# Attention heads of the first mixer: a written order for TensorE, a longer gap in the latent heads' chains, and part of the output projection between their last steps

## The chip, the cores and the metric

The kernel runs on one core of a Trainium2 chip. The metric is device time of one execution in microseconds (us); lower is better. A core has four compute engines that work side by side, each through its own queue in order: TensorE (PE in the profile; its weight loads are shown as PEld), VectorE (DVE), ScalarE (ACT) and GpSimd (POOL). The sync engine (SP) issues the DMA transfers. An instruction at the head of a queue that waits for another engine or for a transfer holds everything behind it on its own engine.

## The reference

One step of a two-layer diffusion backbone on 128 context tokens and 128 latent tokens (`NT` = 256 columns in all), in float32 with a width of 2048. Layer 0 mixes with two groups of heads in parallel, layer 1 with differential attention, and each layer ends in a gated convolution MLP. What this change touches is the mixer of layer 0, after its input projection:

```python
qa = (rmsnorm(q_lat, g_q) @ w_q_up).reshape(b, t, MLA_HEADS, MLA_NOPE_DIM + MLA_ROPE_DIM)
...
kv = (ckv_all @ w_kv_up).reshape(b, s, MLA_HEADS, MLA_NOPE_DIM + MLA_V_DIM)
ka = jnp.concatenate([kv[..., :MLA_NOPE_DIM], krope_all ...], axis=-1)
va = kv[..., MLA_NOPE_DIM:]
out_a = softmax_attention(jnp.concatenate([qa_nope, qa_rope], axis=-1), ka, va, MLA_SCALE)
out_b = softmax_attention(qb, kb_all, vb_all, HEAD_SCALE)
out = jnp.concatenate([out_a.reshape(b, t, -1), out_b.reshape(b, t, -1)], axis=-1) @ w_out
```

There are 8 latent (MLA) heads, whose queries and keys come out of two low-rank products, and 8 grouped-query (GQA) heads, whose queries need a normalisation and a rotation ("rope"). Beside this, all scales and shifts of the layers are computed from a condition vector by a large matrix `w_ada` (its blocks are called units here).

## The kernel before

**Products.** A weight block of 128x128 is split into a high and a low part (`wh` by ACT, `wl` by DVE), the activations likewise, and each block costs three matmuls of 256 columns: `wh` with the high part, `wh` with the low part, `wl` with the high part. A `gemm` sums 4, 6 or 16 blocks in a PSUM bank (`acc`).

**The heads.** They are done in four pairs (h = 0, 2, 4, 6). For a pair come two products for the latent queries (18 matmuls each), one for their rotary part, then for each of two GQA heads its scores (`gqa`) and a product for the latent keys (12 matmuls of 384 columns), then 36 matmuls for the latent values, then the scores of the two latent heads (`mla_pair`). A head's chain is a generator, `head_ab`: row maxima on DVE (`mx`), their scaled negative on POOL (`nmx`), the exponentials on ACT, a reciprocal and two scalings on DVE (`p`); after two hooks the transposes of `p` on PE, after one more the product with the values, whose result is split into `hx`, the operand of the output projection. A hook is a call of `pump`, which stands after each product: it advances each chain by a step, issues some of the matmuls that sum `w_ada` units on PE, and advances a list of `w_ada` sums on DVE (class `Deep`, L525: one custom instruction of 1024 elements; its tiles `block`, `kvb` and `more` are filled by DMAs). How much is set by `RATE` and `SIDE`.

**Query preparation.** `gqa_query(h + 1)` is started before the scores of head h. Its second step issues two small matmuls (`misc`) and the rotation of that head's query, five instructions on DVE. The scores of head h + 1 need it.

**PSUM banks.** Scores, transposes and value products share three banks (`att`), used in turn in the order in which the program asks for them. A tile thus waits until the tile three places before it has been read.

**Order.** In the heads the planner, which simulates the program, chooses the order on every engine from what it believes to be ready. Where `pe.in_turn` is set, PE keeps the order of the code (`keep_order`). In this stage it is not set.

**Output projection.** After the last chain (`flush`) `out_ab` loads three weight tiles and runs the first three of its 16 columns side by side (`first_three`), in the order `PAIR_LATE`: blocks 8 to 15, which are the GQA heads, then blocks 0 to 5, then 6 and 7, the last pair of latent heads. The planner is free to put parts of them between the last chains.

**Pushes.** In the mixer of layer 1, `push` makes two later matmuls wider than 256 columns after each attention step of a head: the first by 32 columns and the thirteenth by 16. The extra columns are not used.

## Time and profile before

| | |
|---|---|
| median of 3 runs | 2304.95 us (2304.35 to 2306.54) |
| the profiled execution | 2307.52 us, of which the span of instructions is 2305.7 us |
| PE busy | 2275.9 us (99%) |
| DVE busy | 1885.6 us (82%) |
| ACT busy | 1195.7 us (52%) |
| granted TensorE clock, mean | 0.993 |
| heads and first three output columns | about 203 to 357 us |
| output projection to its end | to about 438 us |

A row of the timeline gives start, length, engine, line, what is written and read, and how many instructions are merged in it. Matmuls overlap in the records, so what a matmul costs in a dense stretch is the distance from its start to the next start, and the lengths add up to more than the time. A window row gives the busy time of each engine in a stretch with the number of its instructions in brackets, then the granted TensorE clock (1.00 is full speed), the share of the DMA engines and GB/s. The line numbers are those of the kernel before; a short matmul in full float32 (scores, value products, `w_ada` sums) is written once in the code and appears twice in the trace.

### The profile page before, as it was taken

The page shows a single profiled execution, that of the slowest core. Times are in us where ns is not written, and L with a number is a line of the kernel's source. Part 1 is how long each engine was busy: PE and PEld are TensorE (multiplying, and loading weights), DVE is VectorE, ACT ScalarE, POOL GpSimd, SP SyncE. Part 2 cuts the span into 40 slices and gives each one's busy share as a digit, 9 for nine tenths or more (in the row PEclk, how much of TensorE's full clock was granted, in tenths as well). Part 3 has the DMA queues.
Part 4 walks back from the last instruction along what each step waited for, and adds up shares of the span by engine and source line. Part 5 has one row for each costly group of instructions (what it writes and reads, how often), then busy time and mean ns, then how long its engine had stood idle before and what let it go on. Part 6 is the DMA issues. An engine that isn't in the chain of part 4 may idle for free.

```text
span 2305.7 us, 47484 instructions
## 1 busy us (share of the span) xinstructions
PE 2275.9 (99%) x19496; PEld 2182.1 (95%) x19496; DVE 1885.6 (82%) x2973; ACT 1195.7 (52%) x1959; POOL 188.1 (8%) x238
## 2 busy tenths in 40 slices
PE   8999999999999999999999999999999999999998
PEld 6788878999999999999999999999999999999998
DVE  4667979989999999999978988898899965666654
ACT  4345555665553355555575455457555434555543
POOL 0002111300000000001130001023000000000011
PEclk9999999999999999999999999999999999999999
DMA  9987888777777777777788888776667755555553
GB/s 376 367 343 293 326 311 338 288 277 264 262 255 291 291 272 260 272 258 258 288 293 293 318 322 310 267 268 229 246 256 262 264 200 189 199 191 194 198 189 126
DMA packets 100122, 617.15 MB, mean 268 GB/s; under 512 B 10752, under 2 KB 18880, under 8 KB 33344
## 3 DMA queue, kind: packets, MB, share of 16 engines
q1 hardware_dynamic: 99904, 614.11, 72.2%
q8 instruction: 153, 2.51, 0.4%
q14 instruction: 65, 0.53, 0.1%
HBM read 609.32 MB, written 4.75 MB: 266 GB/s over the span
## 4 chain that ended last, share of the span: by engine, by line
PE 93%; DVE 3%; DMA 2%; issue 1%; POOL 1%; ACT 1%; SPq 0%; DVEq 0%; ACTq 0%; POOLq 0%
PE acc L110 86%; PE ada L110 3%; PE att L110 2%; DVE wl L249 1%; DVE hx L525 1%; DMA more<-w_ada 1%; PE att L113 1%; DMA raw<-w_out_c 0%; PE misc L110 0%; DMA araw<-w_ada 0%; DMA kvb<-w_ada 0%; POOL dev L807 0%; PE ada L113 0%; DVE rope L858 0%; ACT wh L248 0%
## 5 line engine op out<-in xcount | busy, mean ns | idle before, releaser
L110 PE MATMUL acc<-hx,wh 128*128 128x256 f32 (+1 forms) x7264 | 1255.2, 278 | 4.2 <-ACT wh L248 1.7
L248 ACT CAST wh<-raw 128x1024 fp32r<-128x1024 f32 (+1 forms) x834 | 796.6, 967 | 869.8 <-PE acc L110 736.6
L249 DVE TENSOR_TENSOR wl<-raw,wh 128x1024 fp32r<-128x1024 f32 (+1 forms) x834 | 925.4, 1126 | 246.9 <-ACT wh L248 240.2
L110 PEld LDWEIGHTS acc<-hx,wh 128*128 128x128 f32 x7264 | 1099.8, 188 | 23.2 <-ACT wh L248 8.1
L110 PE MATMUL acc<-hx,wl 128*128 128x256 f32 (+1 forms) x3632 | 1007.8, 278 | 5.3 <-DVE wl L249 5.1
L110 PEld LDWEIGHTS acc<-hx,wl 128*128 128x128 f32 x3632 | 684.5, 188 | 9.5 <-DVE wl L249 6.9
L110 PE MATMUL acc<-g,wh 128*128 128x256 f32 x2816 | 478.8, 276 | 0.0
L110 PEld LDWEIGHTS acc<-g,wh 128*128 128x128 f32 x2816 | 424.0, 188 | 0.0
L110 PE MATMUL acc<-g,wl 128*128 128x256 f32 x1408 | 388.1, 276 | 0.0
L473 DVE CUSTOM_DVE_ANT_0 junk<-araw,condb 128x2048 f32<-128x2048 f32 x128 | 294.4, 2300 | 0.0
L110 PEld LDWEIGHTS acc<-g,wl 128*128 128x128 f32 x1408 | 264.2, 188 | 0.0
L211 POOL TENSOR_TENSOR sqacc<-sqacc,sq 128x256 f32<-128x256 f32 x62 | 71.5, 1154 | 1491.1 <-ACT sq L207 1490.9
L110 PE MATMUL acc<-hxc,wh 128*128 128x256 f32 (+1 forms) x1056 | 189.3, 281 | 0.0
L110 PEld LDWEIGHTS acc<-hxc,wh 128*128 128x128 f32 x1056 | 161.9, 188 | 1.8 <-issue 1.7
L110 PE MATMUL acc<-hxc,wl 128*128 128x256 f32 (+1 forms) x528 | 146.9, 278 | 0.0
L110 PEld LDWEIGHTS acc<-hxc,wl 128*128 128x128 f32 x528 | 99.6, 189 | 0.2
L110 PE MATMUL acc<-wh,hxc 128*128 128x256 f32 (+1 forms) x512 | 95.0, 283 | 0.5 <-DVE nt L818 0.5
L1531 ACT ACTIVATE cv<-acc,convw 128x256 f32<-128x256 f32 x169 | 94.1, 557 | 0.0
L525 DVE CUSTOM_DVE_ANT_0 hx<-block,condb 128x1024 fp32r<-128x1024 f32 x65 | 79.3, 1221 | 7.3 <-DMA block<-w_ada 6.8
L1537 DVE SCALAR_TENSOR_TENSOR cv<-acc,convw,cv 128x254 f32<-128x254 f32 x169 | 81.1, 480 | 3.2
L843 DVE SCALAR_TENSOR_TENSOR x<-acc,mod,x 128x128 f32<-128x128 f32 x190 | 57.3, 344 | 31.6 <-PE acc L110 31.6
L110 PEld LDWEIGHTS acc<-wh,hxc 128*128 128x128 f32 x512 | 79.4, 188 | 3.4 <-issue 2.5
(263 smaller groups left out, 1800.4 us busy)
## 6 DMA issues: line engine op xcount, KB each, us to landing
raw<-w_up SPq DMA_DIRECT2D x176, 1024.0 KB, 4.8
araw<-w_ada SPq DMA_DIRECT2D x136, 1024.0 KB, 6.0
raw<-w_down SPq DMA_DIRECT2D x88, 1024.0 KB, 4.8
raw<-w_in_c SPq DMA_DIRECT2D x48, 1024.0 KB, 6.9
block<-w_ada SPq DMA_DIRECT2D x41, 512.0 KB, 6.8
raw<-w_in_ab SPq DMA_DIRECT2D x18, 1024.0 KB, 9.1
raw<-w_out_ab SPq DMA_DIRECT2D x16, 1024.0 KB, 7.9
raw<-w_out_c SPq DMA_DIRECT2D x16, 1024.0 KB, 7.1
```

The costliest lines, as they stand in the source:

```text
L110: return self.placed(nc.tensor.matmul(*a, **kw))
L113: return self.placed(nc.tensor.transpose(*a, **kw))
L211: eng.tensor_tensor(out=st["acc"], in0=st["acc"], in1=sq, op=ALU.add)
L248: pin(act.copy(out_hi, src))
L249: pin(dve.tensor_tensor(out=out_lo, in0=src, in1=out_hi.bitcast(F32), op=ALU.subtract))
L473: keep_order(dve.tensor_tensor_reduce(out=T_(feat["pool"], [P, D], "junk"), in1=feat["row"][:, c], in0=feat["raw"].rearrange("p g n -> p ( ...
L525: keep_order(dve.tensor_tensor_reduce(out=self.junk, in0=self.raw, in1=self.row[:, c].rearrange("p (g n) -> p g n", g=2), scale=1.0, scala ...
L843: dve.scalar_tensor_tensor(out=x[:, c, s], in0=ps[:, s], scalar=mod[:, l, 3 * which + 2, c, g:g + 1], in1=x[:, c, s], op0=ALU.mult, op1=AL ...
L1531: pin(act.activation(y, ps, AF.Identity, scale=cw[:, 1, m:m + 1], bias=cw[:, 3, m:m + 1]))
L1537: pin(dve.scalar_tensor_tensor(out=y3[:, :, :T - 1], in0=p3[:, :, 1:], scalar=cw[:, 2, m:m + 1], in1=y3[:, :, :T - 1], op0=ALU.mult, op1=A ...
```

## The change

1. In the heads `pe.in_turn` is set, so PE keeps the order of the code.
2. The chains of the latent heads wait three hooks instead of two before their transposes.
3. `first_three` becomes a class, `Three`. The three weight tiles of the output projection are loaded and two of them split in the last pair (h = 6). After the last scores PE runs 20 blocks (60 matmuls) of the output projection, then the last two heads' transposes, 4 more blocks, the last two value products, and the remaining 24 blocks. Between them stand four calls that advance the DVE sums, whose tile for unused results moves to `qb`.
4. The fourth weight tile of the output projection is loaded before that, and split in the first two of its columns (`W.ahead`).
5. `RATE` of the last quarter of the input projection goes from 0.25 to 0.3, of the heads from 0.72 to 0.62, of the output projection from 0.62 to 0.66: the same `w_ada` matmuls at other places.
6. The first push of layer 1 is 16 columns wide instead of 32.

```diff
-RATE = {"in0": 0.35, "in": 0.5, "in3": 0.25, "heads": 0.72, "out0": 0.62, "c": 0.36, "outc": 0.36}
+RATE = {"in0": 0.35, "in": 0.5, "in3": 0.3, "heads": 0.62, "out0": 0.66, "c": 0.36, "outc": 0.36}
...
-PUSH = [32] + 11 * [0] + [16]
+PUSH = [16] + 11 * [0] + [16]
...
+    class Three:
+
+        def __init__(self, W, xh, xl, order):
+            self.W, self.xh, self.xl, self.order = W, xh, xl, list(order)
+            self.raws = [W.load()[0] for _ in range(3)]
+            self.blocks, self.count, self.ps = {}, [0] * 3, []
+
+        def prepare(self, c, h):
+            self.blocks[c, h] = self.W.halves(self.raws[c], 8 * h)
+
+        def banks(self):
+            self.ps = [T_(pacc, [P, 512], "acc")[:, :NT] for _ in range(3)]
+
+        def run(self, n):
+            for _ in range(n):
+                c, k = self.order.pop(0)
+                if (c, k // 8) not in self.blocks:
+                    self.prepare(c, k // 8)
...
+        def even(self):
+            while isinstance(self.steps[0], partial) and self.steps[0].func == self.sums and self.steps[0].args[-1]:
                 self.step()
...
-    def head_ab(pl, s, rs, v, hx, c):
+    def head_ab(pl, s, rs, v, hx, c, wait=2):
...
-        yield
-        yield
+        for _ in range(wait):
+            yield
         pT = transposed(pl, p)
...
-                        start(head_ab(hp, s[i], rsm, lambda b, i=i: vm[:, b, i], o, h + i))
+                        start(head_ab(hp, s[i], rsm, lambda b, i=i: vm[:, b, i], o, h + i, 3))
...
+                pe.in_turn = True
                 for h in range(0, 8, 2):
...
+                    if h == 6:
+                        W = Weights(A["w_out_ab"], KD, 1)
+                        three = Three(W, lambda k: o[:, k, :NT], lambda k: o[:, k, NT:2 * NT], PAIR_LATE)
+                        three.prepare(0, 1)
+                        three.prepare(1, 1)
                     mla_pair(h, qr, kn, values())
-                flush()
+                deep.junk = qb[:, 0:4].rearrange("p (a b) n -> p a (b n)", a=2)
+                three.banks()
+                step()
+                three.prepare(2, 1)
+                three.prepare(0, 0)
+                for n in (6, 7, 7):
+                    three.run(n)
+                    deep.pump()
+                    if n == 6:
+                        step()
+                step()
+                three.run(4)
+                step()
+                deep.pump()
+                deep.even()
+                W.begun.append(W.load())
+                three.run(len(three.order))
+                pe.in_turn = False
...
-        ready = first_three(W, oh, ol, PAIR_LATE, first=1)
...
+            if c < 2:
+                W.ahead(lambda i: i)
```

In the rows of the changed kernel that follow, line numbers are its own (L883 and L884 are the maxima, L867 and L868 before).

PE, where the last GQA heads (6 and 7) end, before: `att_3682` and `att_3741` are their scores, `att_3773` the transposes of the first one's `p`, `ada_3623` a `w_ada` unit, `acc_3947` the first output column.

```order
L110 MATMUL att_3682<-kg_118,qb_242 128x128
L110 MATMUL att_3682<-kg_118,qb_242 128x256
L110 MATMUL att_3741<-kg_118,qb_242 128x128
L110 MATMUL att_3741<-kg_118,qb_242 128x256
L113 MATMUL att_3773<-cst_74,p_3687 128x128 x3
L110 MATMUL ada_3623<-araw_3632,condw_79 32x512 x4
L110 MATMUL ada_3623<-araw_3677,condw_79 32x512 x4
L110 MATMUL att_3823<-pT_3777,vg_119 128x128 x3
L113 MATMUL att_3829<-cst_74,p_3746 128x128 x3
```

PE, the end of the heads after the change: `acc_3918` is the third output column, `att_4001` and `att_4007` the transposes of the last two latent heads (ahead of them stand 24 matmuls each of the first two columns and 12 of the third, behind them 12 more of the third).

```order
L110 MATMUL acc_3918<-hx_2396,wl_3920 128x256
L113 MATMUL ada_4156<-cst_74,am_4152 128x128 x3
L113 MATMUL att_4001<-cst_74,p_3890 128x128
L113 MATMUL ada_4156<-cst_74,am_4152 128x128
L113 MATMUL att_4001<-cst_74,p_3890 128x128 x2
L113 MATMUL att_4007<-cst_74,p_3904 128x128 x3
L110 MATMUL acc_3918<-hx_2396,wh_3919 128x256 x2
```

Before, the two pairs of scores stand next to each other with no product behind them until the first transposes; after, each wait of a chain has products of the output projection or of the next pair in it.

PE, the second pair of GQA heads (2 and 3), before: `att_2921` and `att_2983` are their scores; they stand a few matmuls apart, in the next pair's latent queries (`acc_3164`).

```order
L110 MATMUL att_2921<-kg_118,qb_242 128x128
L110 MATMUL att_2921<-kg_118,qb_242 128x256
L110 MATMUL acc_3095<-wh_2944,kv_in_1786 128x256
L110 MATMUL acc_3164<-ql_1787,wh_3156 128x256 x2
L110 MATMUL acc_3164<-ql_1787,wl_3157 128x256
L110 MATMUL acc_3164<-ql_1787,wh_3156 128x256 x2
L110 MATMUL att_2983<-kg_118,qb_242 128x128
L110 MATMUL att_2983<-kg_118,qb_242 128x256
```

The same heads after: their scores are now `att_2909` and `att_2983`. Between them stand the product for the latent keys (`acc_2936`), the value products of the latent heads of the pair before (`att_2951`, `att_2957`) and the small matmuls of head 3's query (`misc_2963`).

```order
L110 MATMUL acc_2936<-kv_in_1786,wl_2929 128x384
L110 MATMUL att_2951<-pT_2883,vm_2663 128x128 x3
L110 MATMUL att_2957<-pT_2889,vm_2663 128x128 x3
L110 MATMUL misc_2963<-cst_74,sq_2906 128x1 x2
L110 MATMUL att_2983<-kg_118,qb_242 128x128
L110 MATMUL att_2983<-kg_118,qb_242 128x256
```

`att_2983` now follows `misc_2963` directly, and its bank is that of `att_2909`, three tiles before it.

DVE, after the change, at the same place: `rope_2971` and the two rows behind it are the rotation that `att_2983` needs.

```order
L883 TENSOR_REDUCE mx_2912<-att_2909 128x1
L884 TENSOR_REDUCE mx_2912<-att_2909 128x1
L249 TENSOR_TENSOR hx_2396<-att_2951,hx_2396 128x256
L877 TENSOR_TENSOR qr_2870<-qr_2870,rope_2872 128x128
L459 TENSOR_TENSOR mod_77<-mod_77,cst_74 128x8
L219 TENSOR_SCALAR rv_2966<-misc_2963 128x2
L249 TENSOR_TENSOR hx_2396<-att_2957,hx_2396 128x256
L874 TENSOR_TENSOR rope_2971<-qb_242,cst_74 64x128 x2
L876 TENSOR_TENSOR qb_242<-qb_242,cst_74 128x128
L877 TENSOR_TENSOR qb_242<-qb_242,rope_2971 128x128
```

In the order before, the same rotation stands right behind the scaling of the latent heads' `p`, and five `w_ada` sums follow it before the maxima of `att_2921`:

```order
L905 TENSOR_SCALAR p_2770<-p_2770,rec_2778 128x256
L858 TENSOR_TENSOR rope_2971<-qb_242,cst_74 64x128 x2
L860 TENSOR_TENSOR qb_242<-qb_242,cst_74 128x128
L861 TENSOR_TENSOR qb_242<-qb_242,rope_2971 128x128
L249 TENSOR_TENSOR wl_3250<-raw_3247,wh_3249 128x1024
```

The rotation has moved from well ahead of the scores to behind the maxima of the neighbouring head and the splits of two value products.

More of the change, by code (lines that the diff above doesn't have):

```diff
@@ L331, in last_tile, with first_three @@
             return self.tiles[-1]
-    def first_three(W, xh, xl, order, mid=None, fixed=False, first=0):
-        pin = keep_order if fixed else lambda i: i
-        raws = [W.load()[0] for _ in range(3)]
-        ps = [T_(pacc, [P, 512], "acc") for _ in range(3)]
-        blocks = {(c, h): W.halves(raws[c], 8 * h) for c, h in ((0, first), (1, first), (2, first), (0, 1 - first))}
-        count = [0] * 3
-        for n, (c, k) in enumerate(order):
-            if mid and n == len(order) // 2:
-                mid()
-            if (c, k // 8) not in blocks:
-                blocks[c, k // 8] = W.halves(raws[c], k // 8 * 8)
-            wh, wl = blocks[c, k // 8][k % 8]
-            a, b = count[c] == 0, count[c] == KD - 1
-            count[c] += 1
-            pin(pe.matmul(ps[c][:, :NT], wh, xh(k), start=a, stop=False))
-            pin(pe.matmul(ps[c][:, :NT], wh, xl(k), start=False, stop=False))
-            pin(pe.matmul(ps[c][:, :NT], wl, xh(k), start=False, stop=b))
-        return [p[:, :NT] for p in ps]
+    class Three:
[12 more added lines that the diff above has]
+                    self.prepare(c, k // 8)
+                wh, wl = self.blocks[c, k // 8][k % 8]
+                a, b = self.count[c] == 0, self.count[c] == KD - 1
+                self.count[c] += 1
+                pe.matmul(self.ps[c], wh, self.xh(k), start=a, stop=False)
+                pe.matmul(self.ps[c], wh, self.xl(k), start=False, stop=False)
+                pe.matmul(self.ps[c], wl, self.xh(k), start=False, stop=b)
+    def first_three(W, xh, xl, order):
+        three = Three(W, xh, xl, order)
+        three.banks()
+        for c, h in ((0, 0), (1, 0), (2, 0), (0, 1)):
+            three.prepare(c, h)
+        three.run(len(order))
+        return three.ps
     push = []
@@ L547, in flush @@
             while self.steps:
+                self.step()
+        def even(self):
+            while isinstance(self.steps[0], partial) and self.steps[0].func == self.sums and self.steps[0].args[-1]:
                 self.step()
@@ L1305, in mixer_ab, with out_ab @@
                         pump(RATE["heads"])
-                    mla_pair(h, qr, kn, values())
-                flush()
-        return o
-    def out_ab(o, st, u, beside, rp):
+                    if h == 6:
[3 more added lines that the diff above has]
+                        three.prepare(1, 1)
+                    mla_pair(h, qr, kn, values())
+                deep.junk = qb[:, 0:4].rearrange("p (a b) n -> p a (b n)", a=2)
+                three.banks()
+                step()
[14 more added lines that the diff above has]
+                pe.in_turn = False
+                assert not chains
+        return o, W, three.ps
+    def out_ab(o, W, ready, st, u, beside, rp):
         l = 0
@@ L1315, in out_ab @@
         ada["pew"] = PEW["out0"]
-        W = Weights(A["w_out_ab"], KD, 1)
         oh, ol = (lambda k: o[:, k, :NT]), (lambda k: o[:, k, NT:2 * NT])
@@ L1604, in step_kernel @@
         with tc.tile_pool(name="beside", bufs=1) as beside:
-            o = mixer_ab(hx, beside)
+            o, *begun = mixer_ab(hx, beside)
             with tc.tile_pool(name="raw", bufs=1) as rp:
@@ L1608, in step_kernel @@
                 u = raw_tile(rp, "u")
-                out_ab(o, st, u, beside, rp)
+                out_ab(o, *begun, st, u, beside, rp)
                 W = Weights(A["w_up"][0], KD, 1)
```

## The prediction

> **What bounds the kernel now.** I read the page first, then a table of windows over the heads, then PE's and DVE's timeline where the table shows PE short of work. The page's first rows:

> ```profile
> PE 2275.9 (99%) x19496; PEld 2182.1 (95%) x19496; DVE 1885.6 (82%) x2973; ACT 1195.7 (52%) x1959; POOL 188.1 (8%) x238
> ```

> PE is the bound, so only time in which PE stands still or runs slowly can be won. The windows of the heads:

> ```profile
> core 0: us, PE busy (x) PEld busy (x) DVE busy (x) ACT busy (x) POOL busy (x), PEclk, DMA share, GB/s
> 240.40:277.70 37.30, 36.73 (x271) 30.95 (x268) 34.05 (x88) 18.21 (x47) 8.61 (x14) 1.00 0.89 342
> ...
> 326.90:331.90 5.00, 0.46 (x4) 0.09 (x2) 3.76 (x11) 1.78 (x7) 1.84 (x4) 0.80 0.93 360
> 331.90:336.30 4.40, 4.40 (x20) 1.08 (x20) 4.03 (x11) 0.78 (x3) 0.00 (x0) 0.50 0.50 133
> ...
> 342.50:356.60 14.10, 13.21 (x103) 11.90 (x102) 9.42 (x24) 7.60 (x19) 1.95 (x4) 1.00 0.48 174
> ```

> Two readings. In a whole pair of heads (240.4 to 277.7) PE is busy, and so is DVE with 34.05 of 37.3 us: DVE has a tenth to spare. And behind the last GQA scores PE does next to nothing for 5 us, then runs 4.4 us at a clock of 0.50. In rows of PE's timeline:

> ```profile
> 326.42 0.92 PE L110 MATMUL att<-kg,qb 128*128 128x128 f32 x4 [0.21 <-DVE hx L249]
> 331.88 0.87 PE L113 MATMUL att<-cst,p 128*128 128x128 f32 x3 [4.54 <-DVE p L904]
> 332.68 3.64 PE L110 MATMUL ada<-araw,condw 128*32 128x512 f32 x16
> 336.26 1.16 PE L110 MATMUL att<-pT,vg 128*128 128x128 f32 x6
> ...
> 347.09 0.39 PE L110 MATMUL acc<-hx,wl 128*128 128x256 f32 x1 [0.72 <-DVE wl L249]
> ```

> The transposes wait 4.54 us for `p` of the GQA head scored just before them. What PE's work costs elsewhere in the heads, from start to start:

> ```profile
> 255.23 0.83 PE L110 MATMUL att<-pT,vm 128*128 128x128 f32 x6
> 256.00 1.92 PE L110 MATMUL ada<-araw,condw 128*32 128x512 f32 x16
> 257.85 0.92 PE L110 MATMUL att<-kg,qb 128*128 128x128 f32 x4
> 258.42 0.47 PE L110 MATMUL acc<-wh,kv_in 128*128 128x256 f32 x1
> 258.73 0.40 PE L110 MATMUL acc<-ql,wh 128*128 128x256 f32 x2
> ...
> 262.27 0.39 PE L110 MATMUL acc<-ql,wh 128*128 128x256 f32 x2
> 262.50 0.28 PE L110 MATMUL acc<-ql,wl 128*128 128x256 f32 x1
> 262.61 0.39 PE L110 MATMUL acc<-ql,wh 128*128 128x256 f32 x2
> ```

> Three 256-column matmuls take 0.34 us, 0.113 each; 16 sums 1.85 us; six short ones 0.77 us with the change of work; a pair of GQA scores 0.57 us. And DVE's prices, with the chain from maxima to `p`:

> ```profile
> 327.75 0.29 DVE L867 TENSOR_REDUCE mx<-att 128x1 f32<-128x128 f32 x1
> 327.96 0.42 DVE L868 TENSOR_REDUCE mx<-att 128x1 f32<-128x256 f32 x1
> 328.29 0.28 DVE L867 TENSOR_REDUCE mx<-att 128x1 f32<-128x128 f32 x1
> 328.49 0.42 DVE L868 TENSOR_REDUCE mx<-att 128x1 f32<-128x256 f32 x1
> 328.82 1.22 DVE L525 CUSTOM_DVE_ANT_0 hx<-block,condb 128x1024 fp32r<-128x1024 f32 x1
> 329.95 0.09 DVE L525 DVE_READ_ACCUMULATOR2_ANT mod<- 128x1 f32 x1
> 331.25 0.17 DVE L903 RECIPROCAL rec<-sums 128x2 f32<-128x2 f32 x1 [1.21 <-ACT p L875]
> 331.45 0.29 DVE L904 TENSOR_SCALAR p<-p,rec 128x128 f32<-128x128 f32 x1
> 331.65 0.35 DVE L905 TENSOR_SCALAR p<-p,rec 128x256 f32<-128x256 f32 x1
> ...
> 251.26 0.59 DVE L858 TENSOR_TENSOR rope<-qb,cst 64x128 f32<-64x128 f32 x2
> 251.89 0.29 DVE L860 TENSOR_TENSOR qb<-qb,cst 128x128 f32<-128x128 f32 x1
> 252.21 0.29 DVE L861 TENSOR_TENSOR qb<-qb,rope 128x128 f32<-128x128 f32 x1
> 252.42 1.22 DVE L249 TENSOR_TENSOR wl<-raw,wh 128x1024 fp32r<-128x1024 f32 x1
> ```

> Instructions overlap a little: a pair of maxima costs 0.54 us, a `w_ada` sum 1.13, a query's rotation 1.16. From the end of a head's maxima (328.38) to its reciprocal (331.25) pass 2.9 us, through POOL and ACT.

> **The change, part by part.**

> *The tail (parts 3 and 4).* What goes: the wait of 4.54 us, since PE now always has a product between scores and transposes; the half clock behind it, 16 sums in 3.58 us (332.68 to 336.26) where 1.85 is their price, 1.7 us; and the loss from 342.5 to 356.6, where 103 matmuls at 0.113 would take 11.7 us of 14.1, 2.4 us. Sum 8.6 us. What takes their place: the last scores are followed by 60 matmuls, 6.8 us, before the transposes. The chain needs two pairs of maxima (1.1 us), 2.9 us to the reciprocal, two `p` pairs (about 1.0) and, between them on DVE, two sums (2.3, of which part lies in the 2.9). That is 5.0 to 7.3 us, so 6.8 us of matmuls covers it but for 0.5 at worst; I take 0. The weight splits for the rest stand on DVE behind `p` and ahead of their use by 12 matmuls, the transposes and the value products, 3 us; two half splits take 2.4. The weight loads, three tiles in the last pair and one behind, go past `w_ada` tiles on SP's queue: taken at nothing, since DMA runs at 0.48 of its share from 342.5 to 356.6, and they used to go there or before it anyway. What is late next if they aren't on time is the third column's split.

> *The written order (part 1), where it costs.* PE now stands before the scores of the second GQA head until its query is rotated and its bank is free, and everything of PE is queued behind. From the end of the latent scores PE has, up to that point, 54 matmuls at 0.113 (6.1 us), 12 with 384 columns (estimated at 1.5 times 0.113, 2.0), 16 sums (1.85) and 30 short ones at 0.113 (3.4): 13.4 us. DVE has in the same stretch, in the second pair, four sums (4.6), three and a half splits (4.0), three pairs of maxima (1.6), two `p` pairs (0.9), eleven rotation instructions (2.7) and small ones (1.2): 15.0 us until the rotation is done. The bank comes free 2.9 us behind the maxima of the first head, which end at 12.7: 15.6. So PE waits 2.2 us. In the third pair DVE has a sum more but two splits fewer and the rotation earlier; the bank decides, at 12.3 + 2.9 less 13.4, 1.8 us. In the fourth pair a sum and another half split stand ahead and PE has 16 sums more: 17.5 less 15.3, 2.2 us. In the first pair the rotation is queued long before and three banks lie between: 0. Sum 6.2 us. The same sum with each DVE instruction at its full length (1.22 a sum and a split, 0.71 a pair of maxima) adds 2 us a pair, so the upper end is 12; the lower end is 0, if the DVE work that stands ahead is done in the slack before. I take 6.2, since the rows show DVE instructions overlapping.

> *The written order, where it saves.* Before, short matmuls break the products into small pieces; counted in the two orders, PE changes from one kind of tile to another 115 times in this stage, now 84 times. A return costs about 0.1 us: scores and the first matmul behind them run from 257.85 to 258.73, 0.88 us, where 0.66 and 0.113 are their prices by columns. Some 16 returns fewer: 1.6 us (0 if all of it is hidden in waits).

> *Part 2, the third hook.* The latent heads' transposes stand 54 matmuls and 16 sums behind their scores, 8.0 us, against 7.3 for the chain as above: no wait.

> *Part 5.* The `w_ada` matmuls are the same in number; moved inside stages in which PE is the bound they cost what they cost: 0.

> *Part 6, the pushes.* A stretch behind attention runs slowly until something restores the pace:

> ```profile
> 1268.00:1275.00 7.00, 7.00 (x62) 7.00 (x61) 6.91 (x12) 3.48 (x5) 0.00 (x1) 1.00 0.89 327
> 1324.00:1331.00 7.00, 7.00 (x64) 7.00 (x63) 6.54 (x12) 4.40 (x11) 0.00 (x0) 1.00 1.03 395
> ```

> 62 against 64 matmuls in 7 us is 3%. The pushes on PE's timeline, in another head:

> ```profile
> 1201.60 0.48 PE L110 MATMUL acc<-wh,hxc 128*128 128x288 f32 x1
> ...
> 1205.34 0.41 PE L110 MATMUL acc<-hxc,wh 128*128 128x272 f32 x2
> ```

> From the first push (288 wide) to the second (272) pass up to 3.7 us; if 16 columns restore the pace at once, that is 0.11 us, and with 16 pushes 1.8 us. If they don't, 0; if they upset the second one, as much is lost. I take 1.0 won.

> *Sum:* -8.6 + 6.2 - 1.6 - 1.0 = -5.0 us. The profiled execution took 2307.52 us, 1.8 more than its span and 2.6 more than the median of 2304.95; taken off the median, 2300 us. About 0.2% (4.6 us) is what a measurement of this kernel can tell from no change, so this forecast lies at that line.

> **The clock.** The row at 331.88 shows a wait of 4.54 us, and the window behind it the clock at 0.50. [...]

> **Rivals.**

> *The new waits are hidden.* If DVE is ahead by the time the rotation is called, for which its spare tenth speaks (3.2 us in that pair), the 6.2 us go: 2293.8 us. Against it, the rotation now stands behind the value products' splits, which wait for PE itself.

> *The waits eat the gain.* With the waits at the upper end, 12 us, the sum is +0.8: 2305.7 us. For it, DVE instructions at full length; against it, their overlap.

> *DVE is held by a transfer and PE with it.* In the chain of waits stand

> ```profile
> 256.95 4.09 DMA block<-w_ada
> ...
> 336.81 7.84 DMA kvb<-w_ada
> ```

> A DVE sum whose tile is late holds the rotation, the maxima and the scaling behind it; PE used to have a product to go on with, and now stands. A held sum of 4.1 us behind a wait of 2 makes it pass the 4.5 us at which the clock was seen at half, for another 1.7: 5.8 us. Two of them decide: -5.0 + 11.6 = +6.6, 2311.6 us. For it, DMA shares of 0.89 and 0.93 in this stage; against it, that sums are fewer per pair at the planned rate and wait in spare time too.

> *The pushes do nothing:* 2301 us, inside the forecast.

> **How the numbers follow.** Forecast (2297 to 2303): 0.36, of which 0.19 lies below 2300.3. Hidden waits (2291 to 2297): 0.33. Waits that eat the gain (2303 to 2309): 0.08. Held transfers (2309.5 to 2318): 0.23. So faster by over 0.2% is 0.19 + 0.33 = 0.52; within 0.2% 0.17 + 0.08 = 0.25; slower 0.23. Leaving out the fastest 0.05 of the second case and the slowest 0.12 of the last, the range is 2292 to 2312; the forecast's own is 2297 to 2303.

> **What would show each step.** The 4.54 us wait for `p` and the clock below 1.00 near 332 us gone, and the last two heads' transposes without a wait longer than 0.5 us: the tail is right. PE waits of 1.5 to 2.5 us at the second GQA scores of pairs two to four, released by DVE's rotation or ACT's exponentials: the written order's cost is right; none: the first rival. Waits above 4 us with DVE idle for `block` or `kvb`: the third. Behind the first push, 0.113 a matmul instead of 0.118: part 6. The forecast is wrong if the three output columns' end does not move ahead by 4 us or more, or if something beyond the output projection, where nothing is changed but the pushes, moves by more than 2 us.

## The result

The changed kernel takes 2325.4 us (2323.92 to 2326.6, four runs) against 2305.05 us before: ratio 1.0087, 95% interval 1.0070 to 1.0105, slower by 20 us. The forecast was 2300 us, the range ended at 2312.

The page's first group, and the waits of TensorE from 200 to 440 us (what waited and its line, what released it, us in all, times, the longest):

```profile
PE 2277.9 (98%) x19496; PEld 2187.6 (94%) x19496; DVE 1887.0 (81%) x2975; ACT 1194.2 (51%) x1961; POOL 186.8 (8%) x238
```

```profile
PE ada L110 <- DMA araw<-w_ada: 10.1, 4, 4.7
PE ada L113 <- ACT am L449: 6.5, 3, 4.0
PE att L110 <- DVE qb L877: 4.1, 2, 2.7
PE att L110 <- DVE hx L249: 1.0, 2, 0.6
```

Before, the one long wait was 4.5 us for `p`. It is gone, and in its place stand waits for transfers of `w_ada`, for the copy of a unit's sums (`am`) and for the rotation (`qb`). Windows of the same run, columns as in the prediction:

```profile
core 0: us, PE busy (x) PEld busy (x) DVE busy (x) ACT busy (x) POOL busy (x), PEclk, DMA share, GB/s
207.00:234.00 27.00, 16.16 (x100) 7.50 (x99) 17.21 (x43) 5.46 (x12) 0.95 (x2) 0.69 0.90 330
...
217.46:219.40 1.94, 1.94 (x8) 0.20 (x8) 1.80 (x7) 0.00 (x0) 0.00 (x0) 0.50 0.96 392
...
342.54:346.60 4.06, 4.06 (x15) 3.91 (x16) 3.10 (x8) 0.92 (x4) 1.25 (x2) 0.62 0.99 403
...
357.00:368.00 11.00, 11.00 (x95) 10.62 (x95) 7.88 (x23) 5.93 (x16) 0.82 (x4) 1.00 0.98 394
```

From 207 to 234 us TensorE works 16.2 us of 27, at a clock of 0.69. The end of the heads (357 to 368) is full, at full clock.

Where the 20 us arise is seen in TensorE's loss: a stretch less what its matmuls would take at their usual distance from start to start (0.113 us for 256 columns, 0.1075 for one row of a `w_ada` sum, of which four start within 0.43, and so on for each shape). It is worked out from the starts in the trace, for the runs below too, and good to about 1 us:

| loss of TensorE, us | 200 to 240 | 240 to 320 | 320 to 370 |
|---|---|---|---|
| before | 1.4 | 6.1 | 12.6 |
| changed | 18.4 | 15.0 | 8.0 |

So +17.0, +8.8 and -4.6; behind 460 us the changed kernel makes up 1.2 us.

**The first pair, +17 us.** Ahead of the first GQA scores the four `w_ada` tiles of one unit are now summed in a row (a sum here is the eight rows of the trace that read one tile `araw`), and between these sums TensorE has nothing else (TensorE's timeline, the number in brackets is the idle time before):

```profile
217.46 1.94 PE L110 MATMUL ada<-araw,condw 128*32 128x512 f32 x8 [3.04 <-DMA araw<-w_ada]
219.88 1.94 PE L110 MATMUL ada<-araw,condw 128*32 128x512 f32 x8 [0.48 <-DMA araw<-w_ada]
226.52 1.94 PE L110 MATMUL ada<-araw,condw 128*32 128x512 f32 x8 [4.70 <-DMA araw<-w_ada]
230.37 1.94 PE L110 MATMUL ada<-araw,condw 128*32 128x512 f32 x8 [1.91 <-DMA araw<-w_ada]
233.01 1.11 PE L113 MATMUL ada<-cst,am 128*128 128x128 f32 x4 [0.71 <-ACT am L449]
```

`araw` has two buffers. On the sync engine's queue the third and the fourth tile are issued when the first and the second sum have read theirs (a row with x2 holds two issues, its length reaches from the first to the second):

```profile
209.12 0.92 SPq L599 DMA_DIRECT2D araw<-w_ada  x2
...
219.45 0.33 SPq L599 DMA_DIRECT2D araw<-w_ada  x1
...
221.88 6.96 SPq L599 DMA_DIRECT2D araw<-w_ada  x2
```

From 219.45 to the third sum at 226.52 pass 7.1 us, from 221.88 to the fourth at 230.37 8.5 us. The two journeys overlap each other and the sums; waits of 4.70 and 1.91 us are left of them on TensorE. The sums between them run at a clock of 0.50.

**A wait that goes through four engines.** The wait of 4.0 us for `am`, in the third pair, in rows of DVE, ACT and TensorE:

```profile
289.61 1.23 DVE L537 CUSTOM_DVE_ANT_0 hx<-kvb,condb 128x1024 fp32r<-128x1024 f32 x1 [2.33 <-DMA kvb<-w_ada]
290.76 0.08 DVE L537 DVE_READ_ACCUMULATOR2_ANT mod<- 128x1 f32 x1
290.76 0.29 DVE L883 TENSOR_REDUCE mx<-att 128x1 f32<-128x128 f32 x1
```

```profile
293.13 0.46 ACT L891 ACTIVATE p<-att,nmx,rsmla 128x128 f32<-128x128 f32 x1 [7.88 <-POOL nmx L889]
...
295.36 2.00 ACT L248 CAST wh<-raw 128x1024 fp32r<-128x1024 f32 x2
...
297.51 0.61 ACT L449 COPY am<-ada 128x512 f32<-128x512 f32 x1
```

```profile
298.18 0.66 PE L113 MATMUL ada<-cst,am 128*128 128x128 f32 x4 [4.02 <-ACT am L449]
```

A DVE sum waits 2.33 us for its tile; the maxima of the latent heads stand behind it; ACT waits 7.88 us for their negative (POOL is between); the copy of a unit's sums stands on ACT behind the exponentials and behind two weight casts of 2.00 us; and the unit's transposes stand on TensorE where the code has them, with the next product behind them. How much of the 4.02 us goes back to the late tile, and how much to the casts and to DVE's sum itself, was not tested.

### The profile page after: what moved, and what is told of

Same layout as the page of the kernel before. It is cut to its first block, busy times and chain, and to the rows that moved or that the text cites. A ratio compares the mean times of both kernels' runs of the same rounds, so it can differ in the third digit from the quotient of the medians.

```text
span 2324.5 us, 47468 instructions
## 1 busy us (share of the span) xinstructions
PE 2277.9 (98%) x19496; PEld 2187.6 (94%) x19496; DVE 1887.0 (81%) x2975; ACT 1194.2 (51%) x1961; POOL 186.8 (8%) x238
## 4 chain that ended last, share of the span: by engine, by line
PE 83%; DVE 1%; POOL 1%; DMA 0%; ACT 0%; issue 0%; DVEq 0%; ACTq 0%
PE acc L110 80%; PE att L110 1%; PE ada L110 1%; DMA block<-w_ada 0%; DVE hx L537 0%; POOL dev L823 0%; PE att L113 0%; DVE wl L249 0%; PE ada L113 0%; DVE x L1678 0%; POOL hxc L827 0%; DVE rope L874 0%; DVE dev L815 0%; ACT p L891 0%; DVE hx L249 0%
## 5 line engine op out<-in xcount | busy, mean ns | idle before, releaser
L110 PE MATMUL acc<-hx,wh 128*128 128x256 f32 (+1 forms) x7264 | 1254.1, 278 | 4.2 <-ACT wh L248 1.7
L249 DVE TENSOR_TENSOR wl<-raw,wh 128x1024 fp32r<-128x1024 f32 (+1 forms) x836 | 923.1, 1120 | 254.7 <-ACT wh L248 249.8
L110 PEld LDWEIGHTS acc<-hx,wh 128*128 128x128 f32 x7264 | 1100.0, 188 | 22.4 <-ACT wh L248 8.1
L110 PE MATMUL acc<-hx,wl 128*128 128x256 f32 (+1 forms) x3632 | 1007.4, 277 | 4.3 <-DVE wl L249 4.3
L110 PEld LDWEIGHTS acc<-hx,wl 128*128 128x128 f32 x3632 | 684.4, 188 | 5.6 <-DVE wl L249 5.5
L110 PE MATMUL acc<-g,wh 128*128 128x256 f32 x2816 | 478.8, 276 | 0.0
L110 PEld LDWEIGHTS acc<-g,wh 128*128 128x128 f32 x2816 | 423.7, 188 | 0.0
L110 PE MATMUL acc<-g,wl 128*128 128x256 f32 x1408 | 388.0, 276 | 0.0
L485 DVE CUSTOM_DVE_ANT_0 junk<-araw,condb 128x2048 f32<-128x2048 f32 x128 | 294.2, 2298 | 0.0
L110 PEld LDWEIGHTS acc<-g,wl 128*128 128x128 f32 x1408 | 264.2, 188 | 0.0
L110 PE MATMUL acc<-hxc,wh 128*128 128x256 f32 (+1 forms) x1056 | 188.0, 280 | 0.0
L110 PEld LDWEIGHTS acc<-hxc,wh 128*128 128x128 f32 x1056 | 161.5, 188 | 1.8 <-issue 1.7
L110 PE MATMUL acc<-hxc,wl 128*128 128x256 f32 (+1 forms) x528 | 146.5, 278 | 0.0
L110 PEld LDWEIGHTS acc<-hxc,wl 128*128 128x128 f32 x528 | 99.4, 188 | 0.1
L110 PE MATMUL acc<-wh,hxc 128*128 128x256 f32 (+1 forms) x512 | 94.8, 282 | 0.8 <-DVE nt L834 0.8
L537 DVE CUSTOM_DVE_ANT_0 hx<-block,condb 128x1024 fp32r<-128x1024 f32 x64 | 78.0, 1218 | 13.1 <-DMA block<-w_ada 12.9
L110 PE MATMUL ada<-araw,condw 128*32 128x512 f32 (+1 forms) x608 | 75.5, 607 | 12.0 <-DMA araw<-w_ada 12.0
```

The source lines that it names most:

```text
L110: return self.placed(nc.tensor.matmul(*a, **kw))
L249: pin(dve.tensor_tensor(out=out_lo, in0=src, in1=out_hi.bitcast(F32), op=ALU.subtract))
L485: keep_order(dve.tensor_tensor_reduce(out=T_(feat["pool"], [P, D], "junk"), in1=feat["row"][:, c], in0=feat["raw"].rearrange("p g n -> p ( ...
L537: keep_order(dve.tensor_tensor_reduce(out=self.junk, in0=self.raw, in1=self.row[:, c].rearrange("p (g n) -> p g n", g=2), scale=1.0, scala ...
```

## The experiments

**One number back.** The changed kernel with the old rate in the last quarter of the input projection.

```diff
-RATE = {..., "in3": 0.3, "heads": 0.62, ...}
+RATE = {..., "in3": 0.25, "heads": 0.62, ...}
```

> The changed kernel with one number put back: the last quarter of the input projection issues w_ada matmuls at 0.25 again (0.3 in the change), so that two sums of a unit stand ahead of the first GQA scores on TensorE, and no longer four. Theory A (four sums in a row, each behind a transfer that is issued only when the buffer of the one before is read, cost the 20 us seen from 210 to 234): the waits for araw go, 2325 - 20 = 2305 us (2302 to 2309), and the rest of the heads loses as before it. Rival B (TensorE in written order is held wherever a unit's sums stand, two as much as four): waits for araw of 8 us or more remain near the first scores, 2315 us or more.

Measured: 2317.51 us, ratio 1.0057 (1.0043 to 1.0071). TensorE's waits from 195 to 440 us:

```profile
PE att L110 <- DVE qb L877: 6.7, 3, 5.0
PE att L110 <- ACT p L891: 3.6, 2, 3.3
PE att L113 <- DVE p L920: 2.8, 1, 2.8
```

No wait for `araw` is left: the row of four is the rate's doing, together with the written order. But only 8 of the 20 us come back. With the stall gone the first pair waits 5.0 us for a rotation instead, and the loss from 200 to 240 us is still 9.1 us. In rows of DVE, with TensorE's scores last:

```profile
218.36 1.23 DVE L537 CUSTOM_DVE_ANT_0 hx<-block,condb 128x1024 fp32r<-128x1024 f32 x1 [2.37 <-DMA block<-w_ada]
...
220.65 1.22 DVE L537 CUSTOM_DVE_ANT_0 hx<-block,condb 128x1024 fp32r<-128x1024 f32 x1
...
225.18 0.29 DVE L877 TENSOR_TENSOR qb<-qb,rope 128x128 f32<-128x128 f32 x1
...
225.53 1.22 PE L110 MATMUL att<-kg,qb 128*128 128x256 f32 x2 [4.97 <-DVE qb L877]
```

Two DVE sums, the first with a late tile, stand ahead of the rotation. Rival B falls, and theory A is right on the cause and wrong on the net. This kernel is the base of the runs below that speak of 2317.5 us.

**The planner's order in the pairs, the written one at the end.**

```diff
-                pe.in_turn = True
                 for h in range(0, 8, 2):
...
+                pe.in_turn = True
                 deep.junk = qb[:, 0:4].rearrange("p (a b) n -> p a (b n)", a=2)
```

> The changed kernel with the order of TensorE left to the planner in the four pairs; from the last scores on the written order stays, and all numbers of the change stay (0.3 in the last quarter of the input projection too). Theory A (the written order of the pairs makes both the stall ahead of the first scores, some 20 us, and the 13 us lost between 240 and 320; the end of the heads gains 8 to 14): 2305 - 8 to 14 = 2291 to 2297 us. Rival B (the rate of 0.3 alone, by loads that come late whatever the order, makes the first stall): 2305 + 20 - 14 = 2311 us, with waits for araw near 220. Rival C (the end gains nothing without the written pairs ahead of it): 2305 us.

Measured: 2304.95 us, 0.9997 (0.9988 to 1.0007). Rival C in its number. Two windows:

```profile
311.00:329.50 18.50, 12.68 (x73) 7.37 (x66) 11.80 (x32) 11.22 (x23) 2.35 (x4) 0.82 0.83 308
332.00:343.00 11.00, 11.00 (x93) 8.88 (x90) 8.98 (x23) 5.55 (x15) 0.82 (x4) 1.00 0.78 297
```

The end (332 to 343) is full, as in the changed kernel. What it won is lost again, most of it from 311 to 329.5, where chain steps stand alone, 12.7 us of work in 18.5; that the planner has used up the pairs' products by then is the likely reason. So the blocks of the out-projection between the last steps gain nothing without the written pairs, although this run has the third hook as well, which by itself gains some 3 us (below). And the rate of 0.3 without the written order makes no stall: no wait for `araw` is left.

**The written order alone.** The kernel before, with TensorE in the code's order in the four pairs and their flush.

```diff
+                pe.in_turn = True
                 for h in range(0, 8, 2):
...
                 flush()
+                pe.in_turn = False
```

> The kernel before with one edit, TensorE in written order in the four pairs and their flush; no blocks of the out-projection are between the last steps, chains wait two hooks, old rates. Theory A: the pairs lose 13 us as in the changed kernel, and the last chains, with no product between their steps, lose some 5 more than before: 2305 + 13 + 5 = 2323 us (2316 to 2328). Rival B (the written order costs only with the new rates and the longer chains): within 5 us of before, 2305 to 2310 us.

Measured: 2318.21 us, 1.0057 (1.0043 to 1.0071): 13 us slower, with neither the new rates nor the longer chains. Its loss is 5.1, 18.9 and 8.2 us in the three stretches. The pairs lose what was expected; the extra 5 us at the end did not come: products of the last pair are left for the end, and the planner put the first columns of the out-projection between the last steps by itself, so that the end is full:

```profile
351.10:362.10 11.00, 11.00 (x98) 11.00 (x97) 7.07 (x18) 6.06 (x17) 0.82 (x4) 1.00 0.71 252
```

**The push alone.** The kernel before with `PUSH = [16] + 11 * [0] + [16]`.

> The kernel before with the first push of layer 1 at 16 columns instead of 32, nothing else. Theory A (the 1.1 us that the changed kernel gains behind 1460 us come from the pushes): 2304 us, 1 us faster. Rival B (the pushes change nothing, a matmul behind the scores still takes 0.118 us until the thirteenth): 2305 us. Rival C (where the 16 columns restore the pace, the thirteenth upsets it): 2306 to 2308 us.

Measured: 2305.69 us, 1.0003 (0.9994 to 1.0012): no difference that can be told. Windows of one head behind its value products, from the first push to ahead of the thirteenth matmul, and behind it:

```profile
1223.80:1225.50 1.70, 1.70 (x17) 1.70 (x17) 1.40 (x3) 0.84 (x4) 0.66 (x2) 1.00 0.95 227
1226.50:1233.00 6.50, 6.50 (x57) 6.50 (x56) 6.39 (x12) 3.41 (x5) 0.00 (x0) 1.00 0.86 268
```

In the starts, the first push of 16 columns behind the value products brings the distance from 0.118 to 0.113 us within four matmuls, in six of the seven heads where it falls, and the thirteenth, also 16 wide, sends it back to 0.118; in the last head it is the other way round. In the changed kernel, which has the same two pushes, it is so in five of the seven heads and the other way round in the last two. Behind the scores 16 columns do nothing at once (0.117 to 0.120 us over the next dozen matmuls in the changed kernel). So rival B is right behind the scores, and rival C behind the value products.

**Sums that need not wait for their tile.** On the base of 2317.5 us:

```diff
-                out=self.junk, in0=self.raw, in1=self.row[:, c].rearrange(...),
+                out=self.junk, in0=self.row[:, 1 - c].rearrange(...) if self.dry else self.raw,
+                in1=self.row[:, c].rearrange(...),
```

> The changed kernel with 0.25 in the last quarter of the input projection (2317.5 us), and in the heads the w_ada sums of DVE read the resident condition row instead of the tile that a transfer fills. The transfers still run, the sums are as many and as long, TensorE's order is the same; the sums' results are left out (their units are not summed from w_ada in this stage). Theory A (a sum whose tile is late holds DVE, behind it stand rotations, maxima and scalings, and TensorE in written order waits for those): TensorE's waits for qb (5.0 and 1.3 us), for p (2.8) and for the bank (3.3) go, 2317.5 - 11 = 2306 us (2303 to 2309). Rival B (DVE has too much work ahead of the rotations, whether its data come in time or not): the waits stay, 2315 to 2318 us.

Measured: 2321.4 us, 1.0069 (1.0052 to 1.0086), above the range of either theory. DVE in the second pair:

```profile
261.94 1.22 DVE L537 CUSTOM_DVE_ANT_0 hx<-condb 128x1024 fp32r<-128x1024 f32 x1
263.08 0.08 DVE L537 DVE_READ_ACCUMULATOR2_ANT mod<- 128x1 f32 x1
263.08 0.28 DVE L880 TENSOR_TENSOR qb<-qb,rope 128x128 f32<-128x128 f32 x1
```

```profile
263.43 1.22 PE L110 MATMUL att<-kg,qb 128*128 128x256 f32 x2 [4.07 <-DVE qb L880]
```

DVE's order is the planner's. Here four sums stand between the maxima of one head (255.59) and the end of the rotation for the next (263.08), where the base has one. The waits stay, so theory A, in the form in which it was put (late tiles), is not borne out. But the run changed two things, DVE's order as well as its waits, so it doesn't clear the tiles.

**Fewer sums, none, and none from the stage before.** On the same base, `SIDE["heads"]` 1.6 to 1.2, then to 0, then `SIDE["in3"]` to 0 as well.

```diff
-SIDE = {"in3": 0.4, "heads": 1.6, ...}
+SIDE = {"in3": 0.0, "heads": 0.0, ...}
```

> The changed kernel with 0.25 in the last quarter of the input projection (2317.5 us) and 1.2 instead of 1.6 w_ada sums of DVE per hook in the heads; what is left is summed behind the heads. Theory A (late transfers hold DVE): with more time between two loads into a buffer most tiles are there when their sum comes, 5 to 11 us less, 2306 to 2313 us, if the sums put off cost nothing behind. Rival B (the amount of DVE's work): some 12 sums of 1.13 us fewer, of which a part lies ahead of a waiting TensorE, 2 to 4 us less, 2313 to 2316 us.

> The changed kernel with 0.25 in the last quarter of the input projection (2317.5 us), and no w_ada sums on DVE in the heads; they are all done behind the heads, where they will hold the rest, so that only the heads are read from this run, not the total. Theory A (sums that stand on DVE ahead of rotations, maxima and scalings, late or not, are what TensorE in written order waits for): the waits for qb and p and the bank (13.1 us in all) fall to 3 us or less, and TensorE's loss from 200 to 370 us falls from 29 to some 12 us. Rival B (a chain from scores to transposes is too long for the products between its steps, sums or not): the waits stay at 8 us or more.

> The changed kernel with 0.25 in the last quarter of the input projection, and no w_ada sums on DVE before the out-projection at all; only the heads are read from this run. With the sums gone from the pairs alone one wait of 4.2 us was left at the first pair's second scores, behind two sums left over from the input projection, for whose tile DVE waited 1.8 us. Theory A (those two sums and their late tile are that wait): it falls to 0.5 us or less, and TensorE's loss from 220 to 230 us from 6.4 to 2 us. Rival B (the rotations of the first pair are late by themselves): 3 us or more remain.

Measured with 1.2: 2325.3 us, 1.0088 (1.0073 to 1.0103). The heads gain at their end alone (loss 9.2, 11.7, 3.3 us against 9.1, 11.8, 8.3), and TensorE stops in the next stage, to which the sums were put off; both theories miss:

```profile
457.43 0.58 PE L110 MATMUL acc<-u,wh 128*128 128x258 f32 x1 [8.33 <-ACT u L738]
```

With no sums in the heads (2373.87 us in all, the sums' work done behind them), the waits from 200 to 370 us:

```profile
PE att L110 <- DVE qb L877: 4.2, 1, 4.2
PE ada L113 <- ACT am L449: 0.7, 1, 0.7
```

and with none from the stage before either (2380.01 us):

```profile
PE ada L113 <- ACT am L449: 0.9, 1, 0.9
PE att L110 <- DVE qb L877: 0.6, 1, 0.6
```

The losses of the last one are 3.2, 3.0 and 1.7 us, 7.9 against 29 for its base and 20 for the kernel before. So TensorE in written order waits for DVE's `w_ada` sums, in the first pair for the two left over; with them gone hardly a wait is left. Theory A holds in this form: the sums, late or not, stand ahead of what TensorE needs. These two runs, of which the last is a single execution, take away the transfers for the sums as well, so how much of it is lateness and how much length stays open. Lateness as such is not new: from 200 to 365 us DVE waits 10.8 us for tiles of `w_ada` in the kernel before and 12.0 in the base; in the kernel before TensorE, in the planner's order, has other work in the meantime.

**The rotation two products earlier.** On the same base, the query of a pair's second GQA head is started at the head of the pair.

```diff
                 for h in range(0, 8, 2):
+                    start(gqa_query(h + 1))
...
-                        if h + i < 7:
+                        if i and h + i < 7:
```

> The changed kernel with 0.25 in the last quarter of the input projection (2317.5 us), and the query of a pair's second GQA head is started at the head of the pair, two products earlier, so that its rotation stands on DVE ahead of the first head's maxima. Theory of the prediction (TensorE waits at the second GQA scores because the rotation moved behind the maxima and the splits): the waits for qb go (6.7 us in all), 2311 us. Theory A (DVE is held by late tiles, wherever the rotation stands): the waits move to the bank or to the first scores, 2315 to 2319 us.

Measured: 2315.39 us, 1.0039 (1.0026 to 1.0052), theory A's number. It is 2 us less than the base, but the two intervals overlap. No wait for `qb` is left, as the prediction's theory wants, and 7.2 us of waits for `p` and 2.2 us for the bank are there in its place:

```profile
PE att L113 <- DVE p L920: 7.2, 4, 3.2
PE att L110 <- ACT p L891: 2.2, 2, 1.9
```

Of the 6.7 us at most some 2 were the rotation's place; the rest came back as waits for other work of DVE and for the bank.

**Two hooks again.** On the same base.

```diff
-                        start(head_ab(hp, s[i], rsm, lambda b, i=i: vm[:, b, i], o, h + i, 3))
+                        start(head_ab(hp, s[i], rsm, lambda b, i=i: vm[:, b, i], o, h + i))
```

> The changed kernel with 0.25 in the last quarter of the input projection (2317.5 us), and the chains of the latent heads wait two hooks again instead of three. If the third hook is needed (two hooks are 36 matmuls and 16 sums, 5.9 us, against a chain of 5.0 to 7.3 us, longer where DVE is held): waits of 1 to 4 us for p at the latent transposes of three pairs, 2320 to 2326 us. If it is not: 2317 us.

Measured: 2335.48 us, 1.0135 (1.0120 to 1.0150), 18 us slower than with three, twice what was expected at most. Most of it shows as waits for the rotation, and not for `p` as expected (200 to 460 us):

```profile
PE att L110 <- DVE qb L877: 17.2, 4, 6.7
PE att L113 <- DVE p L920: 8.0, 4, 4.2
```

In written order the distance in the code is the only slack there is. That a chain which is 4 us late makes the next step late too would explain the waits for `qb`; it was not tested apart.

**The written order in the last pair alone.** On the same base, `pe.in_turn = h == 6` at the head of each pair.

> The changed kernel with 0.25 in the last quarter of the input projection, where TensorE's order is the planner's in the first three pairs and written in the last pair and the end. Theory A (where the written order begins, the planner has used up the products and the chains' last steps come together in front of it, as from 310 to 330 us with the order written from the end alone): the loss moves ahead of the last pair, 2303 to 2307 us. Rival B (it is enough that the last pair keeps products for its chains): the tail's 8 to 10 us are won, 2295 to 2298 us.

Measured: 2317.0 us, 1.0049 (1.0033 to 1.0064). Some of the loss did move ahead of the last pair (4.6, 14.0 and 10.1 us, with waits of 3.6 us at 291 to 295), but the time is 10 us above theory A's range: in the last pair itself waits of 2.2 us for the bank and 4.6 us for the rotation came on top.

**The third hook alone, under the planner.** The kernel before, with `wait=3` for the latent heads; then the same with the first push alone, of 16 columns, behind the value products; then with three hooks for all heads.

```diff
-        yield
-        yield
+        for _ in range(wait):
+            yield
         pT = transposed(pl, p)
```

> The kernel before with three hooks instead of two in the latent heads' chains, nothing else; the planner orders TensorE. In written order the third hook was worth 18 us (2335.5 against 2317.5). Theory A (the planner moves products between a chain's steps by itself): no change, 2303 to 2307 us. Rival B (the planner, too, gains from a later place of the transposes in the code): 2298 to 2302 us.

> The kernel before, where behind the value products of a head of layer 1 only the first matmul is made wider, by 16 columns, and the thirteenth not; behind the scores all stays (32 and 16). Theory A (16 columns behind the value products restore the pace of 0.113 us a matmul at once, and the thirteenth upsets it, as in every head of the run with 16 columns alone): the pace behind the value products is 0.113 to the next head's scores, 1 to 2 us less than before, 2303.5 to 2304.5. Rival B (the pace falls back by itself): 2305.5 us.

> The kernel before with three hooks in the latent heads' chains and only the first push, of 16 columns, behind the value products of layer 1. If the two are independent and both real (2302.1 against 2305.4 for the hook, about 1 us in the trace for the push): 2301 us (2300 to 2302.5). If the hook's gain was a chance of one planned order: 2304 to 2306 us.

> As the run with three hooks and one push, and with three hooks in the chains of the GQA heads too. If a later place of the transposes helps the planner wherever it stands: 2297 to 2300 us. If the GQA heads' chains then end too late for the last pair (their blocks stand first in the out-projection): 2303 to 2310 us.

Measured: 2302.1 us with the hook, 0.9990 (0.9981 to 0.9999); 2305.28 us with the push behind the value products, 1.0000 (0.9991 to 1.0009); 2302.93 us with both, 0.9987 (0.9978 to 0.9996); 2303.87 us with three hooks everywhere, 0.9993 (0.9984 to 1.0002). The hook in the latent heads is worth 2 to 3 us, rival B's side; both intervals end just below 1. With the push it was not the 2301 us expected of two gains that add up. For all heads, 1 us less than before, no gain can be told. The loss of the first of these runs is 2.0, 5.0 and 9.8 us against 1.4, 6.1 and 12.6. The wait of 4.54 us at the end is split into shorter ones, at full clock (1.00 from 326 to 340 and from 341 to 353 us):

```profile
328.73 0.94 PE L110 MATMUL att<-pT,vg 128*128 128x128 f32 x6 [2.03 <-ACT pT L884]
...
345.28 0.61 PE L113 MATMUL att<-cst,p 128*128 128x128 f32 x3 [1.20 <-DVE p L904]
346.88 0.30 PE L113 MATMUL att<-cst,p 128*128 128x128 f32 x1 [0.99 <-ACT u L722]
```

The push behind the value products keeps 0.113 us up to the next scores in six of seven heads, as theory A says, but in the total it can't be told from nothing. The hook, with or without the push, is the version to keep: 2 to 3 us ahead of the kernel before and some 23 ahead of the changed one. Both runs with a clear gain have the same change in the heads, so whether a later place of the transposes helps the planner in general, or this one planned order came out well, stays open.

## Why the prediction was wrong

- **Part 5, "the same in number ... 0": this step failed, with the first pair's "0" behind it.** Counting the matmuls left out where they stand and what they wait for. At a rate of 0.3 all four sums of a unit stand ahead of the first scores, at 0.25 two of them; TensorE's written order leaves nothing else between them; with two buffers the third and fourth tile are asked for only when the first and second have been read. That is the stall from 214 to 233 us: 10.1 us of waits for `araw`, then work at half clock, and a loss 17 us above the kernel before where the step had 0. Either part alone makes no such stall (2317.51 us with the old rate, 2304.95 us with the planner's order in the pairs). The old rate returns only 8 us, since the first pair has a second fault: two DVE sums stand ahead of its rotations and cost 5 us of waiting and the clock behind it (0.50 from 225.53 to 229.00; rows above, and the runs without sums). "The rotation is queued long before" was true of the code and not of DVE's row.
- **The written order's waits at the second GQA scores, 6.2 us.** The size was near: 0.6 and 1.4 us in the second pair, none in the third, 2.7 us in the fourth, 4.8 in all. The cause was not what the step named. The rotation's place is worth about 2 us at most (early query); the rest is the `w_ada` sums on DVE with their transfers, which I had counted as work (15.0 us in the second pair) and not seen as what could be removed.
- **Missing from the sum: the unit's transposes.** 6.5 us of waits for `am` in the changed kernel, of which 4.0 come through the chain of DVE, POOL, ACT and TensorE above. I had looked at the scores and the chains' steps, and not at the `w_ada` units, which in written order are steps that wait as well.
- **The clock behind short waits.** The sum takes waits of about 2 us at their length and has no term for the clock behind them; it should have had one. The wait of 2.69 us in the fourth pair was followed by 4.06 us at a clock of 0.62, some 1.5 us more. In the base run a wait of 1.27 us, with gaps ahead of it, was followed by a clock of 0.54 (rows in the last section).
- **The tail, -8.6 us: right in the place, wrong in the part.** The wait for `p` and the half clock went, and the last chains run without a gap; from 320 to 370 us the gain is 4.6 us, since new waits of 1.78 and 2.69 us lie in the same stretch. But it isn't the blocks between the steps that did it: the written order alone has the same full end, and the blocks without the written order in the pairs gain nothing (2304.95 us). The products fill the end where something kept them from being used before, and the written order, which kept them, cost 13 us in all.
- **Part 2, no wait: right in the changed kernel, by the help of the stall.** The longest wait there is 0.2 us. In the base run, without the stall, the latent transposes of the second pair wait 2.8 us for `p`. The hook is worth much more than the step said: 18 us in written order, and 2 to 3 us under the planner, the one part of the change that gains by itself.
- **"Where it saves", 1.6 us.** No run shows this saving apart from the waits; it stays open.
- **Part 6, 1.0 us won: 0.** Both ways that the step named, restored at once and upset by the second, occur behind the value products. Of the 1.2 us behind 460 us, 0.8 arise behind 1438 us, and the kernel with the written order alone, whose pushes are the old ones, gains 0.8 us in the same place; at most 0.4 us are left for the pushes.
- **The rivals.** The third (a late tile holds DVE and so TensorE, 0.23) had the engine right: its sign, a wait above 4 us with DVE idle for a tile ahead of it, stands in the changed kernel (4.02 us, 2.33 for `kvb`) and in the base (4.97 us, 2.37 for `block`). Its two holds at 5.8 us were too few, and it did not name the row of four tiles on TensorE itself. It sought the cause in late tiles alone; the run without late tiles changed DVE's order too and does not decide this.

## What to carry to other kernels

Before an order is fixed by hand on the engine that bounds, list every instruction whose place it fixes, the side work too, and ask of each what it waits for and how many buffers its data have; a planner that may reorder hides late side work which the fixed order shows in full. A gap at the end of a stage may be there because products were used earlier to fill other gaps; filling it again moves the loss, and only the total tells. Of a change with several parts, the one that only moves a chain's steps further apart was the one worth keeping.

## What the runs showed of the hardware

A wait of less than 3 us was followed by half of TensorE's clock. In the prediction it was 4.54 us; in the changed kernel it was 3.04 us (the sums at 217.46, clock 0.50) and 2.69 us (342.54, 0.62), and in the base run a wait of 1.27 us (293.92, 0.54), with gaps of 0.33 us and more just ahead of it. Waits of 1.44 and 1.78 us in the changed kernel (273.26 and 329.76) left it at 1.00.

```profile
271.81:275.22 3.41, 1.97 (x11) 1.91 (x11) 3.23 (x14) 0.94 (x4) 0.82 (x2) 1.00 0.96 344
275.22:278.63 3.41, 3.41 (x29) 1.93 (x28) 2.57 (x5) 0.73 (x3) 2.42 (x2) 1.00 0.36 145
...
340.08:343.49 3.41, 0.95 (x5) 0.90 (x6) 3.33 (x10) 0.44 (x2) 0.75 (x1) 1.00 0.89 363
343.49:346.90 3.41, 3.41 (x13) 3.31 (x12) 2.24 (x9) 1.22 (x5) 1.25 (x2) 0.50 0.95 381
```

```profile
290.71:294.12 3.41, 1.81 (x14) 1.38 (x13) 3.38 (x10) 2.46 (x8) 0.57 (x2) 1.00 1.01 423
294.12:297.53 3.41, 3.41 (x11) 3.23 (x11) 2.74 (x12) 0.00 (x0) 1.10 (x4) 0.50 0.95 383
```

With 1.97 us of work in a slot the next one had the full clock; with 0.95 and 1.81 us it had half. Counted over the two kernels, from 200 to 440 us, ten slots at full clock have less than 0.9 of work: the four with 0.19 to 0.28 were followed by half clock, five with 0.48 to 0.82 by full clock, and one with 0.72 by half. The slot with the wait of 1.78 us (0.48) is among the five that were spared. The base's slot with 1.81 us (0.53) was not, so these counts give no share of work at which the clock falls.

At a clock of 0.50, in the changed kernel, a matmul of 384 columns took 0.32 us from start to start (343.67 to 346.23), against 0.174 at 1.00 in the kernel before, and 16 sums took 3.58 us against 1.85 (in the prediction). By these numbers a full slot of 3.41 us at half clock costs 1.6 to 1.7 us, an estimate.
